# One DMA transpose per chunk pair for the packed keys and queries of a gated delta rule

## The chip, the cores and the metric

The kernel runs on one core of a Trainium2 chip. The metric is the device time of one execution in microseconds (us). TensorE is called PE here, its weight loads PEld, VectorE DVE, ScalarE ACT, GpSimd POOL; SP is the engine whose queue issues nearly all DMAs of this kernel.

## What is computed

The reference is one step of a two-layer trunk. A layer takes 1024 latent tokens and 128 context tokens, normalises and modulates them, projects them to 3088 columns and runs three branches side by side: windowed attention (A), a chunked gating branch (B) and a bidirectional gated delta rule (C). The outputs are joined, projected, normalised and added to the input. The change lies in C, whose chunks are of 64 tokens:

```python
kb = k * beta[..., None]
a_mat = jnp.where(strict, jnp.einsum('bnihd,bnjhd->bnhij', kb, k) * decay, 0.0)
t_mat = lax.linalg.triangular_solve(a_mat + eye, ...)          # one 64x64 inverse per chunk and head
u = jnp.einsum('bnhij,bnjhd->bnihd', t_mat, v * beta[..., None])
w = jnp.einsum('bnhij,bnjhd->bnihd', t_mat, kb * jnp.exp(gc)[..., None])
a_qk = jnp.einsum('bnihd,bnjhd->bnhij', q, k) * decay
...
v_new = uc - jnp.einsum('bihk,bhkv->bihv', wc, state)
o = jnp.einsum('bihk,bhkv->bihv', qd, state) + jnp.einsum('bhij,bjhv->bihv', aqk, v_new)
state = state * jnp.exp(gl)[:, :, None, None] + jnp.einsum('bjhk,bjhv->bhkv', kd, v_new)
```

The products of keys with keys and of queries with keys need the head dimension on the partitions, so that keys and queries, which lie with tokens on the partitions, must be transposed first.

## The kernel before

The state of both layers' activations stays on the chip: `X` holds the normalised input of nine token tiles (eight latent, one context), split into two fp16 halves. Matmuls of the branches take three products of these halves. Each layer runs two traces that are woven together. The **chain** is branch C: gates and short convolution (`c_gates`, `c_features`), then `scan`. The **fill** is everything else: branch B, the output gate of C, attention, and in layer 0 the modulation weights of layer 1 (`mod`). `merge` draws from the fill as much as each part of the chain declares as idle PE time (the `SHARE` table). At the end of a layer comes `out_layer` (the projection at L1048).

`scan` takes two heads at a time (head group `hg` 0 or 1), and the chunks in pairs: chunk p of the forward direction and chunk 15-p of the backward one lie on the two halves of the partitions. Its stages are:

- **First preparations.** `prep` runs ten times: for the context pair of both head groups, then for the eight latent pairs of group 0. Between the latter, the context's triangular inverse is computed on DVE (`solve`, L496 and L498, 31 steps of two instructions), four steps per preparation. Then `inverses` (L506, L513 to L532) finishes it on PE.
- **Latent solve 0** (`lat_solve`): `diagonals` (L474 to L486) and 31 steps of L496 and L498 again, for group 0.
- **Steps 0**: 18 steps of the recurrence of group 0 (`pre`, `post`), with one preparation of group 1 after every second step, eight in all.
- **Latent solve 1, steps 1** for group 1, with the final norm and gate.

So a layer has 18 preparations and the kernel 36. One `prep` makes fp16 high and low parts of keys and queries, packed in `PK` (128 partitions, four kinds, two heads, 128 columns): ACT at L434 and L435, POOL at L436 and L437, DVE at L438 and L439. PE transposes the eight 128x128 blocks of `PK` into one PSUM bank (L443), ACT copies the bank into SBUF as `PT` (L445), and eight matmuls (L450) form the products of keys and queries with keys, called `kkq`. DVE multiplies them with the decay `E` (L455 to L459) and writes them to `NA` or `NAc` (L461). `gp` is a pool of two buffers, so `PK`, `E` and the masks of a later pair can be made while an earlier one is in work; `PT` has one buffer.

Both the transposed blocks and `kkq` come from `psw()`, PSUM tag "c", which has **one** buffer. `pre` (L552, L555), `inverses` and the final gate use the same bank.

The order of the instructions on each engine isn't the program's: the tile framework simulates the program with its own cost model (L1247) and puts the instructions in the order of that simulation, by priority of trace order. Engines then run their own lists strictly in order, SP's list of DMA issues too.

Of the kernel before, what the change touches and what calls it, by code (L numbers as in the profile page):

```python
# [12 lines left out]
F16 = mybir.dt.float16  # L13
# [8 lines left out]
WS = 16.0  # L22
# [22 lines left out]
def hybrid_trunk(  # L45
# [45 lines left out]
    def psw(cols=512, dt=F32):  # L91
        return bank("c", 1, cols, dt)
# [8 lines left out]
        yield  # L101
        tc.cur_priority = at

    # ---------------- constants
    ident = per.tile([128, 128], F32, name="ident")
    make_identity(nc, ident)
    id16 = per.tile([128, 128], F16, name="id16")
# [29 lines left out]
    m_d = dr.tile([NT * 128, 256], F32, name="m_d")  # L137
    cg_d = dr.tile([2, 128, NT * 128], F32, name="cg_d")

    def rsqrt(dst, src, n):  # L140
        G.tensor_tensor(dst, src, mhalf[:, 0:n], op=ALU.pow)  # L141

    # ---------------- weights: hi and lo halves of WS * w
    def load_w(src, cols, dst=None, q=dma):
        """src: dram [1024, cols] -> fp16 tile [128, 8, 2, cols]"""
        if dst is None:
            dst = wgp.tile([128, 8, 2, 256], F16, tag="wg", name=nm("wg"))
        views = [a.rearrange("(k p) c -> p k c", p=128) for a in (src if isinstance(src, tuple) else (src,))]
        n = cols // len(views)
        for h in range(2):  # L150
            st = stg.tile([128, 4, 256], F32, tag="st", name=nm("st"))
            s = st[:, :, :cols]
            for i, view in enumerate(views):
                q(s[:, :, n * i:n * i + n], view[:, 4 * h:4 * h + 4, :])
            hi = dst[:, 4 * h:4 * h + 4, 0, :cols]
            S_.activation(hi, s, AF.Copy, scale=WS)
            V.scalar_tensor_tensor(dst[:, 4 * h:4 * h + 4, 1, :cols], s, WS, hi,  # L157
                                   op0=ALU.mult, op1=ALU.subtract)
        return dst

    def proj_tok(ps, t, wg, c0=0, n=256):
        """token-major: ps [128 tok, n] = X[t] @ w"""
        i = 0
        for k in range(8):
            for (a, b) in ((0, 0), (0, 1), (1, 0)):
                T.matmul(ps, X[:, t, k, a, :], wg[:, k, b, c0:c0 + n], start=(i == 0), stop=(i == 23))  # L166
                i += 1

    # ---------------- vectors of a layer, features on partitions
    def layer_vectors(l, dma=dma):  # L170
        rows = stg.tile([96, 128], F32, tag="st", name=nm("rows"))
        dma(rows[0:8], g_pre[l].rearrange("(a b) -> a b", b=128))
# [9 lines left out]
        V.tensor_copy(vt, ps[:, 0:75])  # L182
        return vt

    # ---------------- adaLN
    def mod_out():
        return vec.tile([128, 2, 8, 2], F32, tag="AB", name=nm("AB"), bufs=2)

# [65 lines left out]
                    todo = []  # L254
                yield 1

    # ---------------- rmsnorm + shift/scale of a token tile, transposed, hi/lo
    def norm_x(hp, xt, xn, first=False):
        sq = hp.tile([128, DM], F32, tag="hf", name=nm("sq"))
        ss = hp.tile([128, 1], F32, tag="ss", name=nm("ss"))  # L260
# [25 lines left out]
            S_.copy(X[:, t, k, 0, :], hf[:, k])  # L286
            (V if first and t in LOV else G).tensor_tensor(X[:, t, k, 1, :], hf[:, k], X[:, t, k, 0, :], op=ALU.subtract)  # L287

    # ---------------- C: projection, short conv, normalisation
    LATP = 1028  # L290

    def c_features(l, vt, cqk, cv_, cw):
# [54 lines left out]
                        d3 = dst.rearrange("p n (h d) -> p n h d", d=64)  # L347
                        V.tensor_tensor(d3, d3, bc(rn.rearrange("p (n h) -> p n h", h=2), 3, 64), op=ALU.mult)

    # ---------------- C: decay and beta in the pair arrangement  # L350
    def c_gates(l, cp, gp, out):
        GB = cp.tile([128, 2, 2, 9, 4], F32, name=nm("GB"))
        wab = gp.tile([128, 8, 2, 16], F16, name="wab")
# [57 lines left out]
        out.extend((GB, eg, kdf, gh, gl))  # L411
        yield 6.0

    # ---------------- C: gated delta rule, two heads at a time
    def scan(l, cqk, cv_, gates, oacc, ng, NAc, keep, wo, light):
        GB, eg, kdf, gh, gl = gates

# [1 line left out]
            return (r * 9 + p) * 4 + 2 * hg  # L419

        def block(hg, NA, r, p):
            """[128, (strict, scores), 2 heads, 64] of chunk pair p"""
            return NAc[:, :, r, 2 * hg:2 * hg + 2, :] if p == CTX else NA[:, :, 8 * r + p, :, :]

        def prep(ep, hg, NA, p):
            gt = ep.tile([128, 2, 2, 2, 64], F16, tag="gt", name=nm("gt"))
            for i, g in enumerate((gh, gl)):
                g2 = g.rearrange("p (r n h) -> p r n h", r=2, n=9)[:, :, p, 2 * hg:2 * hg + 2]
                G.tensor_tensor(gt[:, i], bc(triIc16, 2, 2), bc(g2, 3, 64), op=ALU.mult)
            PK = ep.tile([128, 4, 2, 128], F16, tag="PK", name=nm("PK"))  # L430
            k2 = cqk[hg][:, p, 1, :].rearrange("p (h d) -> p h d", d=64)
            q2 = cqk[hg][:, p, 0, :].rearrange("p (h d) -> p h d", d=64)
            hl = PK.rearrange("p a h (s d) -> p a h s d", s=2)
            S_.copy(hl[:, 1], bc(k2, 2, 2))  # L434
            S_.copy(hl[:, 3, :, 0], q2)  # L435
            G.tensor_tensor(hl[:, 2], bc(k2, 2, 2), hl[:, 1], op=ALU.subtract)  # L436
            G.tensor_tensor(hl[:, 3, :, 1], q2, hl[:, 3, :, 0], op=ALU.subtract)  # L437
            V.tensor_copy(hl[:, 0, :, 0], hl[:, 1, :, 0])  # L438
            V.tensor_copy(hl[:, 0, :, 1], hl[:, 2, :, 0])  # L439
            pst = psw(1024, F16)  # L440
            for a in range(4):
                for h in range(2):
                    T.transpose(pst[:, (2 * a + h) * 128:(2 * a + h + 1) * 128], PK[:, a, h, :], id16)  # L443
            PT = ep.tile([128, 4, 2, 128], F16, tag="PT", name=nm("PT"), bufs=1)
            S_.copy(PT.rearrange("p a h c -> p (a h c)"), pst)  # L445
            kkq = psw()
            for h in range(2):
                for hb in (0, 64):
                    for a in (1, 2):
                        T.matmul(kkq[hb:hb + 64, 128 * h:128 * h + 128], PT[:, a, h, hb:hb + 64],  # L450
                                 PT[:, 0:4:3, h, hb:hb + 64], start=(a == 1), stop=(a == 2))
            xo = psv()[:, 0:256].rearrange("p (r h c) -> p r h c", r=2, h=2)
            for r in range(2):
                for i in range(2):
                    T.matmul(xo[:, r], triL16[:, r, :], gt[:, i, r], start=(i == 0), stop=False)  # L455
                T.matmul(xo[:, r], idb, bc(mneg[:, r, :], 1, 2), start=False, stop=True)
            E = ep.tile([128, 2, 2, 64], F32, tag="E", name=nm("E"))
            S_.activation(E, xo, AF.Exp)
            G.tensor_tensor(E, E, bc(GB[:, 1, :, p, 2 * hg:2 * hg + 2], 3, 64), op=ALU.mult)  # L459
            for r in range(2):  # L460
                V.tensor_tensor(block(hg, NA, r, p).transpose([0, 2, 1, 3]),  # L461
                                kkq[:, 0:256].rearrange("p (h k c) -> p h k c", h=2, k=2), bc(E[:, r], 2, 2), op=ALU.mult)

        # diagonal 32-blocks, one matrix to a partition; W: [128, r, lanes, 64]
        def diagonals(ep, W, L):
            D = ep[:, 0:64 * L].rearrange("p (n c) -> p n c", c=32)
            for r in range(2):
# [30 lines left out]
                V.tensor_tensor(y3[:, 0:m, m:32], y3[:, 0:m, m:32], t3, op=ALU.subtract)  # L498
                yield 1.0

        # negated transposed inverses of the whole chunks, in the place of the strict parts
        def inverses(ep, W, L, Y):
            PQ = []
            for f in range(2):
# [176 lines left out]
                    load_w(w_out[l, :, 256 * k:256 * k + 256], 256, wo[k])  # L681
                yield cost * share[6]

    # ---------------- C: output norm and gate, transposed, hi/lo
    def c_gate(l, cgp):
        wg = load_w(w_in[l, :, C_CG:C_CG + 256], 256)
        for kt in range(2):
# [44 lines left out]
        for i, ch in enumerate((16, 17) if p == CTX else (p, 15 - p)):  # L732
            dma(mix_d[ch // 2, :, 6:8, :, 64 * (ch % 2):64 * (ch % 2) + 64], oc[:, i])

    # ---------------- B: spatial gating
    pairs = [(0, 1), (2, 3), (4, 5), (6, 7), (8,)]

    def b_branch(l, vt, bp):
# [58 lines left out]
            yield 3.2 * n  # L797

    def b_gate(l, bp, k):
        """128 of the branch's 256 features"""  # L800
        cs = slice(128 * k, 128 * k + 128)
        w = bp.tile([128, 8, 2, 256], F16, name=nm("wb"), bufs=1)
        load_w((w_in[l, :, C_BU + 128 * k:C_BU + 128 * k + 128], w_in[l, :, C_BG + 128 * k:C_BG + 128 * k + 128]), 256, w)
# [31 lines left out]
            yield 2.75 * n  # L835
        out(*prev)

    # ---------------- attention, output projection, residual, next layer's h
    def rope_tile(rp, src, nh, rt):
        """src psum [128, nh*64] -> f32 tile"""  # L840
        n = nh * 64
        a = rp.tile([128, 256], F32, tag="ra", name=nm("ra"), bufs=1)
        u = rp.tile([128, 256], F32, tag="ru", name=nm("ru"), bufs=1)
        s3 = src.rearrange("p (h d) -> p h d", d=64)
        V.tensor_tensor(a[:, 0:n].rearrange("p (h d) -> p h d", d=64), s3, bc(rt[:, 0:64], 1, nh), op=ALU.mult)
        V.tensor_tensor(u[:, 0:n].rearrange("p (h d) -> p h d", d=64), s3, bc(rt[:, 64:128], 1, nh), op=ALU.mult)
        a4 = a[:, 0:n].rearrange("p (g s f) -> p g s f", s=2, f=16)
        u4 = u[:, 0:n].rearrange("p (g s f) -> p g s f", s=2, f=16)
        V.tensor_tensor(a4[:, :, 0, :], a4[:, :, 0, :], u4[:, :, 1, :], op=ALU.add)
        V.tensor_tensor(a4[:, :, 1, :], a4[:, :, 1, :], u4[:, :, 0, :], op=ALU.add)  # L850
        return a
# [221 lines left out]
            for x in todo:  # L1073
                make_h(p2, *x)

    # ================================================================ program
    mp0 = ctx.enter_context(tc.tile_pool(name="mod0", bufs=1))
    csp = silu_cond(mp0)
    vt = layer_vectors(0, nc.scalar.dma_start)
# [18 lines left out]
            make_h(ph, xts[t], t, AB, True)  # L1098

    def merge(chain, fill):  # L1100
        """traces fill's parts between chain's, as many as chain's idle tensor engine time takes"""
        credit = 0.0
        while True:
            at = tc.cur_priority
            tc.cur_priority = at - BOOST
            got = next(chain, None)
            tc.cur_priority += BOOST
            if got is None:
                break
            credit += got  # L1110
            while credit > 0:
                c_ = next(fill, None)
                if c_ is None:
                    credit = -1e9
                else:
                    credit -= c_
        for _ in fill:
            pass
# [132 lines left out]
```

## Time and profile before

| | |
|---|---|
| time, median of 3 runs | 1536.72 us (1533.35 to 1539.61) |
| profiled execution, span of its instructions | 1534.3 us |
| PE busy, modelled | 1388.2 us (90%) |
| DVE busy | 980.7 us (64%) |
| ACT busy | 792.4 us (52%) |
| POOL busy | 654.7 us (43%) |
| mean granted TensorE clock | 0.945 |
| DMA traffic | 123.17 MB, 25.3% of 16 engines' span on SP's queue |

The span runs from the first to the last instruction of one execution. The page gives no other time for that execution; the span lies within the three runs, 2.4 us below their median. Busy shares are averages over stages that differ: the rows further below are cut by stage. Layer 0 has its ten first preparations between 205 and 278 us, its latent solve 0 up to about 340, its steps 0 up to about 530; layer 1 has the first preparations between 957 and 1042 us, latent solve 0 up to about 1105, steps 0 between 1120 and 1250.

### The profile page before, as it was taken

The numbers are of one execution on the slowest core, as the hardware profiler recorded it, in microseconds if no ns is written. First come the engines' busy times: TensorE is split into PE (matmuls) and PEld (weight loads), VectorE is DVE, ScalarE is ACT, GpSimd is POOL, SyncE is SP. The second block draws the span as 40 slices with busy tenths as digits, with TensorE's granted clock in tenths as the row PEclk, the third lists the DMA queues.
The fourth block names the chain that finished last, engine by engine and source line by source line (L and its number), as shares of the span: only waits on it lengthen the run. The fifth ranks groups of instructions, "written<-read, shape, count | busy, mean of one in ns | idle before, by whom it ended". The sixth has DMA issues, their size and how long they took to land.

```text
span 1534.3 us, 39975 instructions
## 1 busy us (share of the span) xinstructions
PE 1388.2 (90%) x16407; PEld 1074.4 (70%) x16407; DVE 980.7 (64%) x2466; ACT 792.4 (52%) x1683; POOL 654.7 (43%) x890
## 2 busy tenths in 40 slices
PE   6899978689999989998999899989799979998897
PEld 2765566366767768777897655778587758877787
DVE  2855789862546695575446677797846578658423
ACT  2733455723766554684434344454568753778211
POOL 0751265323655224573223522652646623458200
PEclk8999999989999988999998999999789979999899
DMA  9331023233223012017432122221002011202643
GB/s 361 93 91 44 19 89 96 62 98 115 79 93 93 18 51 85 9 37 219 149 131 74 31 62 81 65 68 30 13 6 63 15 51 33 76 13 47 191 152 110
DMA packets 139522, 123.17 MB, mean 80 GB/s; under 512 B 50574, under 2 KB 115890, under 8 KB 139338
## 3 DMA queue, kind: packets, MB, share of 16 engines
q1 hardware_dynamic: 139213, 120.58, 25.3%
q8 instruction: 128, 2.10, 0.5%
q14 instruction: 56, 0.46, 0.1%
q10 hardware_dynamic: 125, 0.04, 0.0%
HBM read 95.78 MB, written 24.28 MB: 78 GB/s over the span
## 4 chain that ended last, share of the span: by engine, by line
PE 28%; DVE 13%; issue 3%; ACT 3%; POOL 3%; DMA 2%; SPq 0%; DVEq 0%; POOLq 0%; ACTq 0%
PE ps L1048 10%; PE ps L166 6%; PE ps L308 2%; DVE sv L498 2%; DVE sv L496 2%; PE ps L944 1%; PE ps L949 1%; PE ps L694 1%; DMA mix_d<-oc 1%; PE ps L513 1%; DVE sS L933 1%; PE ps L928 1%; DVE y L315 1%; PE ps L529 1%; PE ps L552 1%
## 5 line engine op out<-in xcount | busy, mean ns | idle before, releaser
L166 PEld LDWEIGHTS <-X 128*128 128x128 f16 x3888 | 350.6, 100 | 81.5 <-issue 16.3
L166 PE MATMUL ps<-wg,X 128*128 128x256 f16 x2592 | 323.6, 278 | 8.8 <-POOL X L287 3.4
L940 POOL TENSOR_TENSOR P<-sS,P 128x512 f16<-128x512 f32 (+2 forms) x144 | 150.3, 1044 | 153.4 <-ACT sS L938 108.0
L1048 PEld LDWEIGHTS <-OTm 128*128 128x128 f16 x1728 | 172.0, 100 | 25.8 <-DMA OTm<-mix_d 3.4
L946 ACT COPY PT<-ps 128x1024 f16<-128x1024 f16 (+2 forms) x144 | 128.6, 893 | 82.2 <-PE ps L944 80.9
L1048 PE MATMUL ps<-wo,OTm 128*128 128x256 f16 x1296 | 152.9, 279 | 2.8 <-DMA OTm<-mix_d 2.8
L308 PE MATMUL ps<-X,wg 128*128 128x512 f16 (+1 forms) x864 | 147.0, 330 | 0.5 <-DVE wg L157 0.5
L933 DVE CUSTOM_DVE_ANT_0 sS<-ps,am 128x512 f32<-128x512 f32 (+2 forms) x144 | 88.0, 611 | 79.4 <-PE ps L929 57.3
L308 PEld LDWEIGHTS <-wg 128*128 128x128 f16 x864 | 74.4, 100 | 68.3 <-issue 2.2
L166 PE MATMUL ps<-wb,X 128*128 128x256 f16 x864 | 109.0, 286 | 5.7 <-DVE th L830 3.9
L937 ACT ACTIVATE P<-sS,nmx 128x512 f16<-128x512 f32 (+2 forms) x144 | 96.2, 668 | 27.0 <-DVE nmx L935 26.2
L944 PE MATMUL ps<-id,P 128*128 128x128 f16 x992 | 91.4, 228 | 16.5 <-DVE OTA L979 10.5
L938 ACT ACTIVATE sS<-sS,nmx 128x512 f32<-128x512 f32 (+2 forms) x144 | 96.5, 670 | 1.5
L141 POOL TENSOR_TENSOR rs<-ms,mhalf 128x1 f32<-128x1 f32 x36 | 20.7, 575 | 176.7 <-DVE ms L1057 107.0
L944 PEld LDWEIGHTS <-P 128*128 128x128 f16 x992 | 66.2, 102 | 28.4 <-issue 15.0
L315 DVE SCALAR_TENSOR_TENSOR y<-zT,cw,y 128x1156 f32<-128x1156 f32 x48 | 68.8, 1434 | 20.4 <-ACT y L313 19.8
L498 DVE TENSOR_TENSOR sv<-sv 128x31 f32<-128x31 f32 (+15 forms) x186 | 79.0, 425 | 3.4
L949 PE MATMUL ps<-Vt,PT 128*128 128x128 f16 (+1 forms) x992 | 70.1, 213 | 10.3 <-ACT PT L946 9.3
L496 DVE TENSOR_TENSOR sv<-sv 128x31 f32<-128x31 f32 (+15 forms) x186 | 76.6, 412 | 3.3
L928 PE MATMUL ps<-Kh,qT 128*128 128x128 f16 (+2 forms) x272 | 63.2, 278 | 13.7 <-DVE mx L933 12.5
L929 PE MATMUL ps<-Kl,qT 128*128 128x128 f16 (+2 forms) x272 | 73.1, 278 | 0.0
L1051 ACT ACTIVATE sq<-ps 128x512 f32<-128x512 f32 x36 | 21.4, 594 | 99.3 <-PE ps L1048 60.3
(282 smaller groups left out, 3064.1 us busy)
## 6 DMA issues: line engine op xcount, KB each, us to landing
st<-in_w_in_dram SPq DMA_DIRECT2D x40, 512.0 KB
st<-in_w_mod_dram SPq DMA_DIRECT2D x32, 512.0 KB
OTm<-mix_d SPq DMA_DIRECT2D x18, 512.0 KB
wm<-in_w_mod_dram SPq DMA_DIRECT2D x16, 512.0 KB
xt<-in_x_sample_dram SPq DMA_DIRECT2D x16, 512.0 KB
st<-in_w_out_dram SPq DMA_DIRECT2D x16, 512.0 KB
mix_d<-OTA SPq DMA_DIRECT2D x36, 128.0 KB
xs<-xt SPq DMA_DIRECT2D x9, 512.0 KB
```

Source lines behind the costliest of these rows:

```text
L166: T.matmul(ps, X[:, t, k, a, :], wg[:, k, b, c0:c0 + n], start=(i == 0), stop=(i == 23))
L308: T.matmul(ps[:, 0:n], wg[:, k, b, 128 * hg:128 * hg + 128], X[:, t0:t1, k, a, :], start=(i == 0), stop=(i == 23))
L496: V.tensor_tensor(t3, m3[:, 0:m, m:m + 1].to_broadcast([128, m, w]), y3[:, m:m + 1, m:32].to_broadcast([128, m, w]), op=ALU.mult)
L498: V.tensor_tensor(y3[:, 0:m, m:32], y3[:, 0:m, m:32], t3, op=ALU.subtract)
L933: V.tensor_tensor_reduce(sS[:, 0:nk], ps[:, 0:nk], mk, 1.0, NEG, ALU.add, ALU.max, accum_out=mx[:, h:h + 1])
L937: S_.activation(P16[:, 0, 0:nk], sS[:, 0:nk], AF.Exp, bias=nmx[:, h:h + 1], scale=0.125)
L938: S_.activation(sS[:, 0:nk], sS[:, 0:nk], AF.Exp, bias=nmx[:, h:h + 1], scale=0.125, accum_out=sm[:, h:h + 1])
L940: G.tensor_tensor(P16[:, 1, 0:nk], sS[:, 0:nk], P16[:, 0, 0:nk], op=ALU.subtract)
L944: T.transpose(pt[:, a, 128 * i:128 * i + 128], P16[:, a, 128 * i:128 * i + 128], id16)
L946: S_.copy(PT[:, :, 0:nk], pt[:, :, 0:nk])
L949: T.matmul(pops[:, 128 * h:128 * h + n], PT[:, a, 128 * j:128 * j + 128], Vt[:, blist[j], kv].rearrange("p s d -> p (s d)")[:, 0:n], start ...
L1048: T.matmul(ps[:, 256 * i:256 * i + 256], OTm[:, k, a, :], w[:, k, b, :], start=(n == 0), stop=(n == 23))
```

## The change

In `prep` the eight transposes, their PSUM tile and the copy are replaced by one transposing DMA from `PK` to `PT`, issued by SP. `PT` takes the pool's two buffers in place of one. The bank "c" now holds only `kkq` in a preparation. Comments and two docstrings are dropped elsewhere (left out here). Line numbers of the changed kernel are two higher than before from L141 to L439, and two lower from L446 on: the `kkq` matmuls are L448, the DVE product L459, the solve L494 and L496.

```diff
@@ -137,12 +137,14 @@
     m_d = dr.tile([NT * 128, 256], F32, name="m_d")
     cg_d = dr.tile([2, 128, NT * 128], F32, name="cg_d")
 
+    turn = nc.sync.dma_start_transpose
+
     def rsqrt(dst, src, n):
...
@@ -437,12 +439,8 @@
             G.tensor_tensor(hl[:, 3, :, 1], q2, hl[:, 3, :, 0], op=ALU.subtract)
             V.tensor_copy(hl[:, 0, :, 0], hl[:, 1, :, 0])
             V.tensor_copy(hl[:, 0, :, 1], hl[:, 2, :, 0])
-            pst = psw(1024, F16)
-            for a in range(4):
-                for h in range(2):
-                    T.transpose(pst[:, (2 * a + h) * 128:(2 * a + h + 1) * 128], PK[:, a, h, :], id16)
-            PT = ep.tile([128, 4, 2, 128], F16, tag="PT", name=nm("PT"), bufs=1)
-            S_.copy(PT.rearrange("p a h c -> p (a h c)"), pst)
+            PT = ep.tile([128, 4, 2, 128], F16, tag="PT", name=nm("PT"))
+            turn(PT.rearrange("p a h c -> p (a h) c"), PK.rearrange("p a h c -> p (a h c)"))
             kkq = psw()
             for h in range(2):
                 for hb in (0, 64):
```

The simulated order moves with it on every engine. Two places:

SP's list at the first preparations of layer 0, before. The names are `rt` for the rope table of a token tile, and `st` for weights on their way to the matmuls (w_in) or to the modulation (w_mod).

```order
L154 DMA st_3050<-in_w_in_dram 128x4x256
L996 DMA rt_2675<-in_rope_dram 128x128
L154 DMA st_3054<-in_w_in_dram 128x4x256
L996 DMA rt_2723<-in_rope_dram 128x128
L996 DMA rt_2821<-in_rope_dram 128x128
L996 DMA rt_2869<-in_rope_dram 128x128
L996 DMA rt_2967<-in_rope_dram 128x128
L241 DMA st_3384<-in_w_mod_dram 128x2x512
```

And now:

```order
L443 DMA_TRANSPOSE PT_2237<-PK_2230 128x8x128
L443 DMA_TRANSPOSE PT_2451<-PK_2444 128x8x128
L156 DMA st_3000<-in_w_in_dram 128x4x256
L994 DMA rt_2696<-in_rope_dram 128x128
L443 DMA_TRANSPOSE PT_2592<-PK_2585 128x8x128
L443 DMA_TRANSPOSE PT_2729<-PK_2722 128x8x128
L994 DMA rt_2785<-in_rope_dram 128x128
L443 DMA_TRANSPOSE PT_2866<-PK_2859 128x8x128
L443 DMA_TRANSPOSE PT_2955<-PK_2948 128x8x128
L994 DMA rt_2833<-in_rope_dram 128x128
```

The transposes stand in pairs between the rope loads, one load to two preparations; the list grows by 36 rows for them in all.

DVE's list at the end of the context solve of layer 1, before. `sv` is the solve's scratch, L506 the transposes behind its last step, L461 the product of a first preparation, L933 a row of attention scores.

```order
L496 TENSOR_TENSOR sv_13568<-sv_13568 128x31
L498 TENSOR_TENSOR sv_13568<-sv_13568 128x31
L506 STREAM_TRANSPOSE sv_13568<-sv_13568 128x32x32 x2
L933 ISA sS_14810,mx_14803<-ps_14807,am 128x128
L933 ISA mx_14803 128x1
L935 SCALAR_TENSOR_TENSOR nmx_14805<-mx_14803,nsk 128x1
L461 TENSOR_TENSOR NA_13406<-ps_14300,E_14316 128x2x2x64 x2
L933 ISA sS_14829,mx_14803<-ps_14826,am 128x128
```

And now:

```order
L847 TENSOR_TENSOR ra_14693<-ra_14693,ru_14694 128x8x16
L848 TENSOR_TENSOR ra_14693<-ra_14693,ru_14694 128x8x16
L496 TENSOR_TENSOR sv_13388<-sv_13388 128x2x30
L494 TENSOR_TENSOR sv_13388<-sv_13388 128x31
L496 TENSOR_TENSOR sv_13388<-sv_13388 128x31
L827 SCALAR_TENSOR_TENSOR th_14783<-th_14783,ps_14734 128x256
L504 STREAM_TRANSPOSE sv_13388<-sv_13388 128x32x32 x2
L828 TENSOR_TENSOR th_14783<-th_14783,ps_14734 128x256
L931 ISA sS_14558,mx_14551<-ps_14555,am 128x128
```

Before, two of the ten products come behind the end of the solve (the other stands 13 rows further on). Now the last of the ten stands 65 rows ahead of the solve's last step.

## Rows read from the trace of the kernel before

**Rows 1.** The page, part 1: busy us, share and instructions of each engine.

```profile
PE 1388.2 (90%) x16407; PEld 1074.4 (70%) x16407; DVE 980.7 (64%) x2466; ACT 792.4 (52%) x1683; POOL 654.7 (43%) x890
```

**Rows 2.** Stretches: each engine's busy us and instructions, granted clock, DMA share, GB/s.

```profile
core 0: us, PE busy (x) PEld busy (x) DVE busy (x) ACT busy (x) POOL busy (x), PEclk, DMA share, GB/s
205.00:225.00 20.00, 14.10 (x163) 11.83 (x161) 14.97 (x40) 12.81 (x37) 18.41 (x33) 1.00 0.26 78
225.00:275.00 50.00, 44.97 (x449) 33.37 (x447) 48.65 (x151) 25.65 (x66) 27.35 (x43) 0.97 0.29 86
292.00:335.00 43.00, 34.47 (x277) 23.12 (x277) 36.14 (x99) 19.70 (x39) 8.82 (x9) 0.81 0.36 108
340.00:460.00 120.00, 116.35 (x1593) 84.54 (x1592) 50.31 (x161) 68.13 (x148) 61.84 (x95) 0.97 0.29 93
983.00:1031.00 48.00, 41.50 (x435) 34.48 (x432) 46.77 (x145) 23.27 (x59) 25.91 (x40) 0.96 0.20 57
1120.00:1250.00 130.00, 115.30 (x1928) 96.05 (x1925) 71.87 (x213) 91.66 (x192) 73.07 (x112) 0.96 0.10 29
```

**Rows 3.** Groups: busy us, mean ns | idle before, releasers; the two removed ones.

```profile
L445 ACT COPY PT<-ps 128x1024 f16<-128x1024 f16 x36 | 36.4, 1011 | 10.7 <-PE ps L443 10.6
...
L443 PE MATMUL ps<-id,PK 128*128 128x128 f16 x288 | 22.8, 221 | 3.3 <-DVE NA L461 2.4 <-DVE PK L439 0.8
```

**Rows 4.** Line 443: durations, first and last start; what its engine waited for.

```profile
L443 PE MATMUL ps<-id,PK x288: 218/219/314, 211.8 to 1235.4; 128*128 128x128 f16 x144
...
  DVE NA L461: 6.8, 10
```

**Rows 5.** Timeline, layer 1, one preparation: start us, us, instruction [idle <-releaser].

```profile
977.31 0.74 DVE L461 TENSOR_TENSOR NAc<-ps,E 128x256 f32<-128x256 f32 x2
...
978.11 0.62 PE L443 MATMUL ps<-id,PK 128*128 128x128 f16 x8
...
980.89 1.00 ACT L445 COPY PT<-ps 128x1024 f16<-128x1024 f16 x1
...
982.82 0.42 PE L450 MATMUL ps<-PT 128*64 128x128 f16 x8
...
986.82 0.74 DVE L461 TENSOR_TENSOR NA<-ps,E 128x256 f32<-128x256 f32 x2
...
987.62 0.62 PE L443 MATMUL ps<-id,PK 128*128 128x128 f16 x8
```

**Rows 6.** Timeline, layer 1: first transposes, and a later pair's packed operands.

```profile
963.07 0.61 PE L443 MATMUL ps<-id,PK 128*128 128x128 f16 x8
...
966.46 0.40 DVE L439 COPY PK<-PK 128x128 f16<-128x128 f16 x1 [0.42 <-POOL PK L436]
```

**Rows 7.** Timeline of DVE, layer 1, from context solve to latent solve.

```profile
1030.70 3.85 DVE L506 STREAM_TRANSPOSE sv<-sv 128x1024 f32<-128x1024 f32 x2
...
1040.86 0.76 DVE L461 TENSOR_TENSOR NA<-ps,E 128x256 f32<-128x256 f32 x2
...
1047.87 2.85 DVE L476 STREAM_TRANSPOSE sv<-NA 32x512 f32<-32x512 f32 x4 [4.82 <-PE ps L529]
...
1056.64 0.20 DVE L496 TENSOR_TENSOR sv<-sv 128x31 f32<-128x31 f32 x1
```

**Rows 8.** Timeline of DVE, layer 0, the same places.

```profile
269.10 3.89 DVE L506 STREAM_TRANSPOSE sv<-sv 128x1024 f32<-128x1024 f32 x2
...
277.25 0.76 DVE L461 TENSOR_TENSOR NA<-ps,E 128x256 f32<-128x256 f32 x2 [1.85 <-PE ps L450]
...
291.62 0.20 DVE L496 TENSOR_TENSOR sv<-sv 128x31 f32<-128x31 f32 x1
```

**Rows 9.** Chain that ended last: start us, us, a 64 KB load's wait.

```profile
1234.08 2.21 DMA rt<-in_rope_dram
```

**Rows 10.** The same chain: a 64 KB store in 128-byte pieces.

```profile
721.70 5.44 DMA mix_d<-oc
```

**Rows 11.** Timeline of SP: the issue of one load.

```profile
354.24 0.42 SPq L891 DMA_DIRECT2D rt<-in_rope_dram  x1
```

## The prediction

> **What bounds the kernel now.** I read the busy shares first, then the same by stretches, then the removed instructions, then one preparation in the timeline, and last the places where a stage ends. PE is busy 90% of the span, DVE 64% [rows 1], so that PE looks like the bound; the stretches say otherwise for 20 of the 36 preparations [rows 2]. In the middle of the first preparations DVE is busy 48.65 of 50 us in layer 0 and 46.77 of 48 in layer 1, while PE idles 5.0 and 6.5 us. There DVE is the bound, since the context solve runs between the preparations. At the very start of layer 0's preparations it is POOL, 18.41 of 20 us. The other 16 preparations lie in steps 0, where PE is busy 116.35 of 120 us in layer 0 and 115.30 of 130 in layer 1: there an instruction less on PE is time.
>
> The timeline shows what orders the first preparations among themselves [rows 5]. A pair's transposes start at 978.11, right after the product of the pair before it (977.31 + 0.74 = 978.05) gave the bank "c" back. Its copy starts at 980.89, its matmuls at 982.82, its product ends at 987.56, and at 987.62 the next transposes start. So the bank goes round in 9.5 us, and 4.7 of these lie between transposes and matmuls. The packed operands were no cause: those of the pair transposed at 978.11 were ready at 966.86 [rows 6], 11 us ahead. PE itself idled 6.8 us in 10 waits for that product [rows 4], little, because fill stands in its list.
>
> **The change part by part.** *Removed on PE.* Eight transposes take 0.62 us [rows 5], which agrees with 22.8 us for 288 [rows 3]. In steps 0 this is 16 x 0.62 = 9.9 us of a nearly full engine, and I take all of it. The 20 others lie under DVE and count nothing; without that cover they would be 12.4 us more.
>
> *Removed on ACT.* 36 copies, 36.4 us [rows 3]. ACT is busy 68.13 of 120 and 91.66 of 130 us in steps 0 [rows 2], so its own time counts nothing. What counts is the link of the chain that the copy was.
>
> *The bank.* It is no longer held from the transposes to the matmuls, so the preparations run ahead of the solve. What this is worth I read at the end of the solve, since DVE is full before it. In layer 0 the solve's last transposes end at 269.10 + 3.89 = 272.99, the last product of the preparations at 277.25 + 0.76 = 278.01 [rows 8]: the chain waits 5.0 us. In layer 1 it is 1034.55 and 1041.62, 7.1 us [rows 7]. Only behind that come the matmuls of the context inverse and, released by them, the diagonals of the latent solve (1047.87). In the new order the last product stands 65 rows of DVE ahead of the solve's end, so this wait should go: 12.1 us. What is then late is the solve itself with its PE part, not a preparation.
>
> *At the start.* The context pairs no longer wait for each other's bank, so the solve can begin earlier. The bounds are 0, since POOL is full in layer 0 [rows 2], and the 4.7 us of one bank cycle per layer. I take 2 per layer, nearer the low end: 4 us.
>
> *Added: 36 transposing DMAs of 256 KB.* No transposing DMA stands in the trace, so I bound its landing, from SP's issue, by other transfers. Below, a plain 64 KB load took 2.21 us [rows 9]. Above, a 64 KB store cut into 128-byte pieces took 5.44 us [rows 10], and at four times the bytes with no overlap this would be 21.8 us. I take about 4 us, nearer the plain load, since whole rows of 2 KB are read. Against that stands the 11 us for which packed operands lay ready; with two buffers of `PT` two transfers can be ahead. So the landing is hidden by what now waits for the bank. Without this cover it would come up 36 times.
>
> By a rule of the Trainium skill the change is wrong. "VectorE: DVE Perf Modes", section "The three transpose paths", prices a 128x128 transpose at 390 ns on TensorE and 1309 ns by DMA, and its rules for kernel authors send it to TensorE where PSUM will do. The trace has 0.62 us for eight on PE, far under the page; no run yet shows the DMA. Eight times 1309 ns would be an estimate of 10.5 us per landing, which belongs to the first rival below.
>
> *Added on SP.* SP's list grows by 36 issues at 0.42 us each [rows 11], 15 us. In it, rope loads and weights now stand behind transposes that wait for `PK` and for a free `PT`. The engines behind these loads are DVE (rope) and PE (modulation). If the issue alone is hidden it costs 0; if all of it shows, 15 us. I take 6: the queue is mostly waiting for its own releases, but the rope loads of the first preparations are used soon after they land.
>
> Sum: -9.9 - 12.1 - 4 + 6 = -20.0 us. Against the profiled execution's span of 1534.3 this gives 1514.3. What lies around the span I set at the 2.4 us by which the median of the runs stands above it, so 1516.7; I say 1517.
>
> **The rivals.** *Hidden anyway.* DVE keeps the first preparations as long as they were, for instance because the fill that no longer fits between them comes right behind the solve; then 12.1 and 4 fall away and -9.9 + 6 stay: 1533. For it: DVE at 97% of both stretches, and fill that is only moved. Against: DVE is not full behind the solve, it waited 1.85 us for the last matmuls in layer 0 [rows 8] and 4.82 for the inverse in layer 1 [rows 7]. A landing of twice the 5.44 us row, 10.9, ends here too: each pair of preparations would go at the pace of its landing, 10.9 + 0.42 = 11.3 us, which is inside what a pair takes now.
>
> *Late landing, the slower side.* The third transpose needs the first `PT` back, so two preparations can't take less than one landing and one set of matmuls. Now two take (278.01 - 211.8) / 5 = 13.2 us in layer 0 [rows 4, 8] and (1041.62 - 963.07) / 5 = 15.7 in layer 1 [rows 6, 7]. PE's list is strict, so that a late `PT` stops all fill behind it. From a landing of 13 us on the change loses. At 16 us, pairs of 16.4 cost 5 x 3.2 + 5 x 0.7 = 19.5 us, the chain's gains are gone, and 19.5 - 9.9 + 6 = +15.6 gives 1552; at 21.8 us it is 5 x 9.0 + 5 x 6.5 - 3.9 = +73.6, or 1610. For it: data of two bytes turned across partitions might go in small pieces, as the store did, and no row shows such a DMA. Against: the packed rows of 2 KB are long, as in the plain load.
>
> *The clock.* Where PE is busy 80%, between 292 and 335, it was granted 0.81 of its 2.4 GHz, a mean over stretches at 1.2 and at 2.4, against 0.97 and 0.96 in the first preparations [rows 2]. With fewer instructions there PE could fall too. Its 86.5 us in both stretches would become 86.5 x 0.965 / 0.81 = 103, of which its idle 11.5 us hide most: +5 in those and as much in the solve behind, 1527.
>
> **How the numbers follow.** Forecast (1517, its own range 1504 to 1529) 0.56; hidden anyway (1533, from 1526 to 1541) 0.23; late landing (1545 to 1610) 0.15; clock (1522 to 1533) 0.06. What a measurement of this kernel can tell from no change is about 0.5%, 7.7 us: faster is below 1529, slower above 1544.4. Faster: 0.56, a quarter of hidden anyway (0.06) and half of the clock, together 0.65. Slower: 0.15. The same: the rest, 0.20. The range reaches from 1496, where the bank is worth its upper bound in both layers and SP costs nothing (-9.9 - 12.1 - 9.4 = -31.4, 1505, and some way under it for a new order of the fill), to 1546, which takes in all of hidden anyway and the beginning of the late landings.
>
> **What would show it.** In the changed profile: no L443 on PE and no L445 on ACT; matmuls of `kkq` that seldom wait for a DMA; products (L459) of the first preparations at intervals of 4 to 6 us and all before the end of the context solve; the latent solves starting 5 and 7 us sooner behind it; steps 0 about 5 us shorter in each layer. I am wrong if PE's or DVE's waits in these stretches name the transposing DMA for more than about 10 us in sum, if a landing is over 10 us, or if the first preparations with the context solve are no shorter and the loads behind the transposes come late.

## The result: 1552 us, 1% slower, and the profile after

The changed kernel takes 1551.92 us (median of 5 runs, 1549.56 to 1555.54), the kernel before 1535.96 beside it (1533.35 to 1539.61): ratio 1.010, interval 1.0075 to 1.0126. I had said 1517, range 1496 to 1546. Both the direction and the range are wrong.

First the page of the changed kernel, which answers to [rows 1]: its span and the line of busy times, and the line of DMA packets (139522 packets and 123.17 MB before).

```profile
span 1550.7 us, 39548 instructions
...
PE 1383.9 (89%) x16119; PEld 1070.3 (69%) x16119; DVE 984.0 (63%) x2466; ACT 758.9 (49%) x1647; POOL 652.0 (42%) x890
...
DMA packets 177536, 132.58 MB, mean 85 GB/s; under 512 B 88590, under 2 KB 153906, under 8 KB 177354
```

PE has lost 288 instructions that took 22.8 us [rows 3], but its busy time fell by 4.3 alone (1388.2 to 1383.9), and its idle time (span less busy) rose from 146.1 to 166.8. The rest is the clock. I add up, over stretches of 10 us, busy time times (1 - granted clock): 64 us before, 76 after. So PE's work without this slow part fell by 16.1, the slow part rose by 11.8 and the idle time by 20.7: +16.4 us of span. (Each comes from one execution.)

The transposing DMA itself (line 443 now), with what it took on SP and who waited for it, where [rows 4] had the transposes:

```profile
L443 SPq DMA_TRANSPOSE PT<-PK x36: 1232/1244/2486, 211.0 to 1222.1; - x36
...
who waited for it (us, times):
  ACT PK L436: 26.7, 15
  PEld L448: 7.2, 7
  PE ps L448: 4.4, 5
```

Each holds SP 1.24 us, against 0.42 for a load [rows 11]. PE waits for it 4.4 us, its weight loads 7.2. ACT waits longer: the next packing can't write `PK` before the DMA has read it.

Then the stages, by stretches that begin and end with the same instructions. Columns as in [rows 2]. Before: steps 0 of layer 0; from the end of layer 1's latent solve to its steps 0; steps 0 of layer 1; steps 1 of layer 1.

```profile
381.50:526.10 144.60, 140.00 (x2030) 106.90 (x2031) 75.71 (x234) 91.45 (x202) 76.19 (x117) 0.99 0.24 74
1100.70:1127.50 26.80, 24.38 (x379) 20.88 (x376) 12.98 (x30) 12.77 (x23) 10.94 (x9) 0.75 0.03 9
1127.50:1244.10 116.60, 104.70 (x1792) 87.34 (x1792) 65.68 (x200) 85.06 (x180) 71.25 (x110) 0.98 0.11 32
1321.60:1414.10 92.50, 86.39 (x1558) 72.14 (x1559) 62.59 (x192) 71.30 (x160) 62.25 (x89) 1.00 0.15 37
```

The same four after:

```profile
387.30:536.90 149.60, 137.16 (x1994) 104.53 (x1994) 77.44 (x240) 84.88 (x195) 73.71 (x114) 0.99 0.31 83
1091.70:1126.50 34.80, 31.59 (x400) 25.00 (x397) 14.23 (x30) 18.67 (x35) 13.82 (x12) 0.59 0.02 5
1126.50:1250.90 124.40, 108.72 (x1778) 91.19 (x1779) 72.03 (x212) 79.60 (x177) 70.87 (x110) 0.94 0.19 43
1331.20:1433.60 102.40, 89.51 (x1529) 73.07 (x1530) 64.19 (x197) 74.76 (x166) 63.77 (x89) 0.95 0.15 38
```

In steps 0 of layer 0 PE does less (137.16 for 140.00) and idles 12.4 us in place of 4.6. In layer 1 the latent solve ends 9 us sooner, and the next stretch, at a granted clock of 0.59 in place of 0.75, uses up all but one of them; steps 0 then take 7.8 us more, and steps 1 another 9.9, the largest loss of all. Layer 0 makes its loss good by its end (its last matmuls end at 811.4 before, 812.4 after); layer 1, where the output layer starts 16.3 us later, does not.

One thing had moved that I had not looked for: the loads of `M`, the first operands of the spatial gate, a piece of the fill (`b_gate`, line 820 now, 822 before). SP's timeline, start and us, before, for the first two of layer 1:

```profile
854.72 0.37 SPq L822 DMA_DIRECT2D M<-m_d  x1
...
859.40 0.36 SPq L822 DMA_DIRECT2D M<-m_d  x1
```

After, and DVE's last product of the first preparations there:

```profile
1008.86 1.02 SPq L820 DMA_DIRECT2D M<-m_d  x2
...
1008.11 0.74 DVE L459 TENSOR_TENSOR NA<-ps,E 128x256 f32<-128x256 f32 x2
```

The first load starts 154 us later, in the moment in which that product ends. The change gave `PT` a second buffer, 2 KB per partition, and I take it that the pool of the preparations now reaches over SBUF that the gate's tiles get afterwards. The runs with other buffers below bear this out.

### The profile page after: what moved, and what is told of

Read it like the earlier page. It is cut to its first block, busy times and chain, and to the rows that moved or that the text cites. A ratio compares the mean times of both kernels' runs of the same rounds, so it can differ in the third digit from the quotient of the medians.

```text
span 1550.7 us, 39548 instructions
## 1 busy us (share of the span) xinstructions
PE 1383.9 (89%) x16119; PEld 1070.3 (69%) x16119; DVE 984.0 (63%) x2466; ACT 758.9 (49%) x1647; POOL 652.0 (42%) x890
## 2 busy tenths in 40 slices
DMA packets 177536, 132.58 MB, mean 85 GB/s; under 512 B 88590, under 2 KB 153906, under 8 KB 177354
## 4 chain that ended last, share of the span: by engine, by line
PE 38%; DVE 11%; ACT 5%; issue 4%; DMA 3%; POOL 2%; SPq 0%; DVEq 0%; POOLq 0%; ACTq 0%
PE ps L1046 11%; PE ps L168 9%; PE ps L310 4%; DVE sv L494 2%; PE ps L942 2%; DVE sv L496 2%; PE ps L692 2%; PE ps L947 1%; ACT PT L944 1%; ACT P L935 1%; PE ps L511 1%; PE ps L527 1%; DMA PT<-PK 1%; PE ps L926 1%; ACT sS L936 1%
## 5 line engine op out<-in xcount | busy, mean ns | idle before, releaser
L168 PEld LDWEIGHTS <-X 128*128 128x128 f16 x3888 | 355.7, 101 | 86.5 <-issue 25.0
L168 PE MATMUL ps<-wg,X 128*128 128x256 f16 x2592 | 330.9, 283 | 11.6 <-POOL X L289 3.3
L494 DVE TENSOR_TENSOR sv<-sv 128x31 f32<-128x31 f32 (+15 forms) x186 | 75.4, 405 | 3.0
L496 DVE TENSOR_TENSOR sv<-sv 128x31 f32<-128x31 f32 (+15 forms) x186 | 74.9, 403 | 3.3
L947 PEld LDWEIGHTS <-PT 128*128 128x128 f16 x992 | 50.4, 102 | 31.0 <-ACT PT L944 22.7
```

The lines of the kernel that those rows point to most:

```text
L494: V.tensor_tensor(t3, m3[:, 0:m, m:m + 1].to_broadcast([128, m, w]), y3[:, m:m + 1, m:32].to_broadcast([128, m, w]), op=ALU.mult)
L947: T.matmul(pops[:, 128 * h:128 * h + n], PT[:, a, 128 * j:128 * j + 128], Vt[:, blist[j], kv].rearrange("p s d -> p (s d)")[:, 0:n], start ...
```

## The experiments

Ratios are to the kernel before, timed beside each; "clock" is the mean granted clock of a kernel's runs (kernel before: 0.948 over 91 runs), "idle" PE's idle us in the profiled execution (146.1 before).

| run | transposes | us | ratio, interval | clock | idle |
|---|---|---|---|---|---|
| the change | DMA | 1551.9 | 1.0100, 1.0075-1.0126 | 0.938 | 166.8 |
| e1 | PE, and DMA into a dead tile | 1553.5 | 1.0118, 1.0066-1.0170 | 0.938 | 156.5 |
| e2 | none | 1533.8 | 0.9986, 0.9966-1.0006 | 0.948 | 159.0 |
| e3 | DMA in the 20 first | 1539.6 | 1.0039, 1.0014-1.0064 | 0.939 | 148.4 |
| e4 | DMA in steps 0 | 1531.0 | 0.9975, 0.9946-1.0003 | 0.946 | 158.0 |
| e5 | PE, dead tile alone | 1546.8 | 1.0076, 1.0049-1.0103 | 0.940 | 154.8 |
| e6 | PE, and plain copies | 1556.1 | 1.0121, 1.0068-1.0175 | 0.936 | 158.3 |
| e7 | PE, and 20 dead DMAs | 1552.8 | 1.0102, 1.0064-1.0141 | 0.937 | 158.6 |
| e8 | DMA issued by ACT | 1542.9 | 1.0042, 1.0018-1.0065 | 0.939 | 158.3 |
| e9 | DMA, one `PT` | 1550.7 | 1.0085, 1.0057-1.0113 | 0.938 | 172.3 |
| e10 | DMA, one `E` and `gt` | 1524.4 | 0.9926, 0.9899-0.9954 | 0.942 | 157.5 |
| e11 | DMA, one `PT` in the first 20 | 1529.3 | 0.9950, 0.9921-0.9980 | 0.944 | 157.8 |
| e12 | PE, dead tile, one `E` and `gt` | 1522.4 | 0.9900, 0.9873-0.9928 | 0.950 | 146.0 |
| e13 | PE, dead tile in the gate | 1549.0 | 1.0089, 1.0056-1.0122 | 0.938 | 158.7 |
| e14 | PE, one `E` and `gt` | 1525.7 | 0.9936, 0.9905-0.9967 | 0.949 | 137.0 |
| e15 | PE, other shares | 1528.7 | 0.9950, 0.9924-0.9975 | 0.946 | 139.6 |
| e16 | e10, other shares | 1540.5 | 1.0034, 1.0007-1.0060 | 0.942 | 166.2 |
| e17 | DMA, gate with one `th`, `ot` | 1554.6 | 1.0131, 1.0096-1.0167 | 0.938 | 169.6 |
| e18 | e4, one `E` and `gt` | 1522.3 | 0.9925, 0.9901-0.9950 | 0.949 | 148.0 |

**Is it the DMA, or the new order?** My first theory A: the list, ordered anew, is worse. Rival B: the DMA costs.

A tile that nothing reads is called dead here. e1, added behind the copy of the kernel before:

```
+ dead = ep.tile([128, 4, 2, 128], F16, tag="dead", name=nm("dead"), bufs=1)
+ nc.sync.dma_start_transpose(dead.rearrange("p a h c -> p (a h) c"), PK.rearrange(...))
```

> The kernel before, with its transposes and copies, and beside them 36 transposing DMAs of PK into a tile that nobody reads. In layer 0 its order of work is that of the kernel before. Theory A (the DMA is hidden, and the loss comes from the new order of the list): 1536 to 1540 us. Rival B (the DMA itself costs: it holds SP for 1.24 us, its 1056 packets hold the queues, and the loads behind it come late): 1546 to 1555, as much as the changed kernel lost.

+18.6 us: it looked like B. e2, in the changed kernel:

```
- PT = ep.tile(...); turn(PT..., PK...)
+ PT = PK
```

> The changed kernel without the transposing DMA: the matmuls read PK untransposed (this leaves the transposition out, so the numbers computed are others). Theory A (new order): no gain worth the name although nothing is transposed by anybody, 1532 to 1552 us. Rival B (the DMA costs): the predicted gain of 26 without SP's share shows, 1508 to 1518.

No gain, as A has it: nobody transposes, and the time is that of the kernel before. Both theories had one run each, so I split by stage, with the transposes and the single `PT` of before in the other branch:

```
e3: if hg == 0 or p == CTX:  <DMA>   else: <as before>
e4: if hg == 1 and p != CTX: <DMA>   else: <as before>
```

> DMA transposes in the 20 first preparations alone; the 16 in steps 0 by TensorE and copy, as before. Rival C (the loss sits in steps 0, where SP waits 55 us for PT with loads behind it): 1520 to 1530 us, the gain of the bank stays and the loss goes. Theory A (new order): anywhere from 1530 to 1555, and not the sum of the parts.

> DMA transposes in the 16 preparations of steps 0 alone; the 20 first ones as before. Rival C: 1545 to 1556 us, all of the loss. Theory A: 1527 to 1545, since the first preparations and the solves keep their order; if PE's 9.9 us count, 1527.

The parts give +4.7 and -3.9 us, and together +16: they don't add up. C, that the loss sits in steps 0, falls, since steps 0 alone lose nothing. e5 decides: it takes the DMA out of e1 and leaves its dead tile.

> The kernel of e1_dead_turn with the dead tile and without the DMA into it: its order of work is that of e1 to the row, on PE, DVE, ACT and POOL, and differs from the kernel before only in layer 1 (the tile takes SBUF). Theory A (the order is what costs): 1550 to 1555 us, as e1. Rival B (the transposing DMA itself costs): 1533 to 1538, as the kernel before, and all of e1's 18 us are the DMA's.

A tile that nothing touches costs 12 us. In it, as in the changed kernel, the `M` loads are late; SP's and DVE's timelines of e5 show the load 1.1 us behind the end of the last product:

```profile
1035.71 0.94 SPq L823 DMA_DIRECT2D M<-m_d  x2
...
1033.88 0.77 DVE L462 TENSOR_TENSOR NA<-ps,E 128x256 f32<-128x256 f32 x2
```

So most of what e1 lost is not the DMA's. e6 keeps that order to the row on all five engines, e7 but for two rows of DVE (e1 differs in at most 40 of PE's 16407):

```
e6: dma(dead, PK)
e7: if hg == 0 or p == CTX: nc.sync.dma_start_transpose(dead..., PK...)
```

> The same order again, and in the place of the transposing DMA a plain copy of PK into the dead tile, 36 times 256 KB. If it is the transposition (1056 packets, SP held 1.24 us) that costs: the time of e5_dead_none, +0 to +4 us. If any DMA there costs (the hold on PK, the place in SP's list): the time of e1, 1550 to 1555.

> The same order again, with the dead transposing DMA in the 20 first preparations alone. If the DMA costs by the piece (theory B): 20/36 of what e1 has over e5_dead_none. If it costs mainly where the preparations follow one another closely (e3 +4.7 against e4 -3.9 us): nearly all of it, over 80%. Theory A: no difference from e5_dead_none.

Over e5 and e13, which are the same order without a DMA (1546.8 and 1549.0), the three with one stand at 1552.8 to 1556.1: 4 to 9 us for the DMAs, each with intervals that overlap; all 13 runs of the three have a mean of 1553.8, the 14 of e5 and e13 one of 1548.5. Plain copies, which hold SP 0.47 us each, cost as much as transposes, so it is not the transposition. That 20 DMAs (e7) cost less than 36 (e1) can't be told from noise. e8 moves the issue: `turn = nc.scalar.dma_start_transpose`.

> The changed kernel with the 36 transposes issued by ACT and not by SP, so that no load stands behind them; the order of the list moves too. Rival SP (the hold on SP's list costs): 1530 to 1540 us. If the DMA's own work or the clock costs, wherever it is issued: 1545 to 1560; above 1560 if ACT's copies and exponentials stand behind the waits that SP had.

9 us less than the change and still slower than before: between the two, in an order of its own, with the `M` loads as late as in the change (1008.9).

**Is it the room?** Theory D, from the `M` loads. Edits in the changed kernel, e12 in e5:

```
e9:  PT = ep.tile(..., bufs=1)
e10, e12: E = ep.tile(..., bufs=1); gt = ep.tile(..., bufs=1)
e11: PT = ep.tile(..., bufs=2 if hg and p != CTX else 1)
```

> The changed kernel with one buffer of PT in place of two, as the kernel before had. Theory D (room: the second PT's 2 KB of SBUF push the tiles of the first preparations over those of the spatial gate, whose first loads of M then wait for the last product, 1008.9 us in place of 854.7 in layer 1): those loads stand early again, and the time is 1522 to 1538 us. Theory A without room (any other order costs) or B (the DMA costs): 1545 to 1556. A single PT makes each transpose wait for the matmuls of the pair before it: if that is dear, above 1540 too, with L448 waiting for the DMA.

> The changed kernel with both buffers of PT, and one in place of two of the small tiles E and gt (2 KB together), so that the first preparations take no more SBUF than before. Theory D (room): M loads early, 1520 to 1538 us. Theories A and B: 1545 to 1556. A single E makes ACT's exponential wait for the product of the pair before it, which may give back some us.

> The changed kernel with one buffer of PT in the 20 first preparations and two in the 16 of steps 0. Theory D: M loads early, 1520 to 1538 us, and not over e9_one_pt. B: 1545 to 1556.

> The kernel of e5_dead_none (the kernel before with a dead tile of 2 KB) with one buffer in place of two for E and gt, so that the room is that of the kernel before again; TensorE transposes, no DMA. Theory D: 1530 to 1540 us, the 12 us of the dead tile are gone. If the dead tile cost only through some other order, by chance: 1545 to 1555 would be as likely.

In all four the first `M` load of layer 1 is early again (866.6, 851.2, 850.2 and 839.1 us). Three are faster than the kernel before, e9 is not: D missed it. PE's waits for the DMA there are 4.4 us, as in the changed kernel. But e9 and e11 differ only in the second `PT` of steps 0, and by 21.4 us. Of the 26.2 us between their profiles 14.6 lie between the first and the last update of the state in steps 0 of layer 1 (e9, then e11):

```profile
1135.11:1269.10 133.99, 112.45 (x1807) 92.95 (x1805) 78.98 (x229) 87.68 (x188) 72.39 (x109) 0.93 0.19 42
1122.31:1241.73 119.42, 103.15 (x1699) 86.29 (x1694) 72.40 (x217) 79.38 (x178) 65.18 (x103) 0.90 0.19 44
```

Whether this is the wait for a free `PT` or one more order, no run tells. e13 makes the overlap from the other side, a dead tile of 2 KB in the gate's pool:

> The kernel before with a dead tile of 2 KB in the pool of the spatial gate, and none in that of the preparations. Its order is to the row that of e5_dead_none, M loads late. Theory D (overlap): 1545 to 1550 us. If e5's 12 us came from the place of the preparations' own tiles: 1533 to 1538.

As D has it: the rows of e13 stand on all five engines as in e5, and the time is e5's. So in the kernel before, this overlap, wherever it comes from, costs 12 to 14 us. The traces also show where. On the five engines e5's order is that of the kernel before up to 1010 us. From the first update of the state in steps 1 of layer 1 to the end of the span, in the kernel before, e5, e17 (below) and the change:

```profile
1330.52:1534.27 203.75, 182.68 (x2392) 156.31 (x2390) 98.14 (x272) 89.85 (x208) 72.28 (x102) 0.97 0.32 97
1335.17:1551.66 216.49, 193.82 (x2500) 165.61 (x2498) 102.35 (x289) 98.05 (x222) 75.99 (x107) 0.95 0.31 93
1326.98:1553.15 226.17, 202.27 (x2593) 171.80 (x2591) 106.96 (x305) 105.12 (x235) 78.50 (x110) 0.96 0.30 90
1341.04:1550.66 209.62, 186.08 (x2386) 158.08 (x2382) 97.42 (x266) 88.22 (x204) 71.03 (x102) 0.95 0.32 95
```

In e5 PE has 108 instructions more left for this stretch, which takes 12.7 us longer, of 17.4 between the two profiles (it is 216.94 us in e13). They are work of the fill that comes too late: attention's last softmax starts 7.5 us behind the last update of the state, where it was 2.7 ahead of it. e17 takes the overlap from the changed kernel by the gate (`th` and `ot` with bufs=1):

> The changed kernel as it is, with one buffer in place of two for the two small tiles th and ot of the spatial gate (2 KB together), so that the gate no longer reaches over the first preparations. Theory D (overlap): M loads early and 1520 to 1538 us. If it is scatter of orders alone: anywhere from 1522 to 1555, and over 1540 speaks against D.

Against D: `M` is loaded at 854.8 and nothing is gained. Its last stretch has the late attention of e5 (10.7 us behind) and costs more. The changed kernel loses 5.9 us there on balance, with its softmax 14.2 us ahead of the last update: its 16 us are not the loss of e5 over again. The overlap is enough to explain e5 and e13, but not the changed kernel.

Over all twenty kernels, `M` is late in the change, e1, e3, e5 to e8 and e13 (1539.6 to 1556.1 us). It is early in the other twelve: nine of them take 1522 to 1536 us, and e9, e16 and e17 take 1540.5 to 1554.6. Late loads go with slow orders, but what they cost differs (4.7 us in e3), and they are not the only way to lose.

**The route alone, and the scatter of orders.** e14 is the kernel before with e10's two edits; e18 is e4 with them; e15 and e16 change numbers of the table of shares:

```
e15: 5.56, 5.93, 4.8, 2.49 -> 5.5, 5.9, 4.75, 2.45
e16: the same four         -> 6.18, 6.55, 5.42, 3.11
```

> The kernel before, with TensorE transposes, and one buffer in place of two for E and gt: the pair of e10_one_e (1524.4, DMA). If the route of the transposes hardly matters (theory D): within 6 us of 1524. If the DMA route gains PE's 9.9 us: 1533 to 1536; if the DMA costs 7 us as in e1 over e5: 1516 to 1519.

> DMA transposes in the 16 preparations of steps 0, TensorE ones in the 20 first, one buffer for E and gt. If the 9.9 us of PE in steps 0 count (e4 was 3.9 us under the kernel before): 1514 to 1521 us. If the route hardly matters: 1522 to 1528, as e10 and e14.

Between e14 and e10, which have the same buffers of `E` and `gt`, the change is worth -1.2 us, which is no difference. But `PT` has one buffer in e14 and two in e10. The pair with the same buffers throughout is the kernel before and e9, and there the DMA costs about 13 us (1.0085). Where orders alone move the time by as much, neither pair gives the worth of the route. The pages of e14 and e10, first with TensorE, then with DMA:

```profile
span 1520.1 us, 40011 instructions
...
PE 1383.1 (91%) x16407; PEld 1069.8 (70%) x16407; DVE 985.2 (65%) x2466; ACT 790.4 (52%) x1683; POOL 651.7 (43%) x890
```

```profile
span 1522.3 us, 39522 instructions
...
PE 1364.8 (90%) x16119; PEld 1057.8 (69%) x16119; DVE 990.2 (65%) x2466; ACT 758.2 (50%) x1647; POOL 651.0 (43%) x890
```

PE works 18.3 us less and idles 20.5 more. Steps 0, where the removed transposes were to count, are no shorter: in layer 0, e14 and then e10 (in layer 1 120.30 and 121.80 us):

```profile
381.10:520.70 139.60, 134.39 (x1992) 102.20 (x1991) 69.26 (x226) 88.79 (x196) 72.42 (x116) 1.00 0.25 77
385.60:532.40 146.80, 135.51 (x1993) 103.42 (x1994) 77.85 (x240) 84.19 (x195) 75.99 (x117) 0.99 0.31 84
```

e18, whose 16 transposes less should count most, agrees with both.

> The kernel before with the preparations' four numbers in the table of shares lower by 0.03 to 0.06 of 1.2 to 5.9: the same instructions and the same room, in another order. If scatter of orders explains differences of 12 us: over 5 us from the kernel before, on either side. If orders at equal room agree: 1531 to 1539 us.

> e10_one_e (DMA, room restored) with the preparations' shares higher by 0.62, the TensorE time of a preparation that is gone, so that as much fill is put there. If the fill was too thin beside the preparations: 1510 to 1520 us. If it is one more order among others: 1520 to 1550.

Nothing but the order differs between e15 and the kernel before (-6 us), or between e16 and e10 (+16): scatter, and not a matter of too thin a fill.

## Why the prediction was wrong

**The step that failed: "16 x 0.62 = 9.9 us of a nearly full engine, and I take all of it".** PE's work did fall, by 16 us in all, and its idle time rose by 20.7. From e14 to e10 it is nearly one for one. The steps took 5.0 and 7.8 us more: in layer 0 with less on PE, in layer 1 with 14 instructions fewer at a lower clock (0.94 for 0.98). That a PE which is busy 97% of a stretch still keeps pace with a chain beside it is how I read this; which chain, no run shows. The first rival, "hidden anyway", at 1533, comes near e2 (1533.8) by luck: it gave up the bank and kept these 9.9 us.

**The bank's 12.1 us: the mechanism was right, the worth was not.** The last product ends at 270.25 and 1008.85, before the context solve's last transposes (271.96 on DVE in layer 0), and the latent solve of layer 1 starts 7.4 us sooner than in [rows 7], as forecast; DVE's timeline after:

```profile
1049.28 0.20 DVE L494 TENSOR_TENSOR sv<-sv 128x31 f32<-128x31 f32 x1
```

In layer 0 it is 0.9 us and not 5.0 (290.73 for 291.62 in [rows 8]), mostly since the context solve itself ends 2.9 us later (275.90). The 7.4 are gone at the start of steps 0, in the stretch shown above. There PE runs slower; granted clock by 10 us, before and then after:

```profile
1080.00:1090.00 10.00, 3.90 (x35) 2.95 (x36) 9.83 (x26) 2.90 (x6) 6.19 (x8) 0.67 0.04 13
1090.00:1100.00 10.00, 8.93 (x80) 6.80 (x78) 9.01 (x29) 8.60 (x18) 3.78 (x4) 0.65 0.03 8
1100.00:1110.00 10.00, 7.58 (x121) 6.70 (x120) 7.88 (x16) 5.85 (x11) 7.37 (x6) 0.86 0.07 21
```

```profile
1080.00:1090.00 10.00, 4.63 (x42) 3.63 (x43) 9.75 (x29) 3.98 (x10) 7.35 (x11) 0.80 0.33 71
1090.00:1100.00 10.00, 6.75 (x85) 5.30 (x84) 8.35 (x19) 8.38 (x15) 7.09 (x7) 0.50 0.01 3
1100.00:1110.00 10.00, 10.00 (x114) 7.47 (x112) 2.90 (x10) 4.44 (x11) 4.87 (x5) 0.50 0.04 15
```

After, the 20 us from 1090 are all at 0.50, the lower level of 1.2 GHz, behind 10 us in which PE was busy 4.63. Before, PE was busy still less in those 10 us (3.90) and was granted more behind them, so this stretch alone does not tell why. The rival on the clock named a slower clock, in another place, and 10 us in all where the slow part grew by 11.8.

**The start's 4 us** came to 1.6 (the context solves begin at 223.7 for 224.1 and 982.1 for 983.3).

**SP's +6 us** was of the right size, 4 to 9 in the order of e5. Its reason stays open: plain copies, with 0.47 us of SP each in place of 1.24, cost as much, so the length of the issue is not it, and no run separates the place in SP's list from the traffic or from the hold on `PK`.

**The landing** I took at 4 us. The profile of e9 states it:

```profile
DMA to landing us min/median/max: 3.1/3.1/3.9
```

The rival of a late landing falls, and so does the estimate of 10.5 us from the Trainium skill ("VectorE: DVE Perf Modes", section "The three transpose paths", 1309 ns for each of eight): a landing takes 3.1 us for all eight, and the measurement decides. What comes late is the issue: in steps 0 the transpose waits for a free `PT`, and ACT's next packing for the transpose. SP's waits for the matmuls that free it (us, times, longest):

```profile
SPq L443 <- PE ps L448: 55.5, 12, 15.7
```

ACT's wait is on the chain of waits of the changed kernel (start, us):

```profile
1138.33 0.37 PE ps L448 x8
1138.77 4.43 DMA PT<-PK
1143.22 0.41 ACT PK L436
```

It is new, and tempting as the cause; but ACT waits 30.1 us in this way in e10, more than the 26.7 above, and e10 is 27 us faster. My sign of being wrong, over about 10 us of PE's or DVE's waits for the DMA, is just met by 4.4 and 7.2 us on PE and its weight loads; the steps, which were to be 5 us shorter, say it more plainly.

**What I left out.** I counted the second `PT` as a help ("two transfers can be ahead") and gave its 2 KB no price. And the sum took the order of all other work as given, where the new order of the list alone is worth -6 (e15) to +14 us (e13).

**What stays open.** Shown: in the changed kernel, and from e14 to e10, the work taken off PE came back as idle time; the same instructions take 1528.7 to 1549.0 us in other orders; the overlap costs the kernel before 12 to 14, at the end of layer 1. Not shown: what the route is worth by itself, and which feature of its order costs the changed kernel 16. The overlap agrees with e10 and e11 and disagrees with e17; e9 has no second `PT` in steps 0. All kernels above 1539 us have a mean clock of 0.936 to 0.940 but e16 (0.942), all under 1535 one of 0.942 to 0.950; whether the clock is cause or consequence there, no run tells.

Faster than both kernels are e10, e12, e14 and e18 (1522 to 1526 us): what they share is one buffer of `E` and `gt`, and e12 and e14 need no transposing DMA. It is not enough: e16 has it too and takes 1540.5.

## What to carry to other kernels

A busy share, even of 97% in a stretch, did not price the removed work here: ask whose wait ends last, and take removed work of an engine as a gain only where you can say why its idle time won't grow. Where a scheduler or SBUF addresses decide the order, price a changed buffer count as an edit of its own, and compare routes at equal buffers, in more than one order. Before a difference of 1% is given a cause, time one or two edits that change the order and nothing else: here they moved the time by as much as the change.

## What the runs showed of the hardware

A transposing DMA of 256 KB inside SBUF lands 3.1 us after its issue (median in e9 and e10, at most 4.5), holds SP 1.24 us, and moves in (177536 - 139522) / 36 = 1056 packets of about 250 bytes; a plain copy of the same tile takes (144706 - 139522) / 36 = 144 packets (page of e6) and cost the kernel no less. And the kernel before, run 91 times, had a mean granted clock between 0.941 and 0.958 and spans between 1523.5 and 1545.2 us; a straight line through them gives 8 us less for each 0.01 of clock, which says what goes together and not which causes which.
